# A branch moved from behind the last expert group to behind the sixth, its loads on another queue, and a shorter lead of split weights

## The chip, the core and the metric

The kernel is written in Bass with Tile for one core of a Trainium2 chip. The metric is device time in microseconds (us) of one execution; the time shown is the median of three runs. TensorE (PE) multiplies, VectorE (DVE) and ScalarE (ACT) do elementwise work, GpSimd (POOL) a little of it, and SyncE (SP) issues the DMAs. [...]

## What is computed

Two transformer blocks run one after the other on 256 tokens of width 1024, all in 32-bit floats. The first block ends in a mixture of experts: each token goes to two of 32 experts.

```python
def hierarchical_moe(h, w_rg, b_rg, w_re, b_re, w_gate, w_up, w_down):
    ...
    for g in range(N_GROUPS):
        sl = slice(g * EXPERTS_PER_GROUP, (g + 1) * EXPERTS_PER_GROUP)
        act = jax.nn.silu(jnp.einsum('nd,edf->nef', h, w_gate[sl])) * jnp.einsum('nd,edf->nef', h, w_up[sl])
        act = act * combine[:, g, :, None]
        y = y + jnp.einsum('nef,efd->nd', act, w_down[sl])
    return y
```

The second block has projections, attention and a gated unit side by side, an output projection, a layer norm, a dense feed-forward net (`swiglu_ffn`) and a second layer norm.

```python
def hybrid_mixer(x, w_in, attn_out_g, gmlp_out_g, gmlp_ln_g, gmlp_ln_b, w_spatial, b_spatial, w_out):
    h = x @ w_in
    q, k, v, u, z = jnp.split(h, [A, 2 * A, 3 * A, 3 * A + G], axis=-1)
    ...
    merged = jnp.concatenate([rms_norm_2(attn, attn_out_g), rms_norm_2(sg, gmlp_out_g)], axis=-1)
    return merged @ w_out
```

## The kernel before, in words

**Weights.** All weights come from HBM in tiles of 1 MB (128 partitions x 2048 floats). `Feed` (lines 53 to 88) keeps one fixed order of tiles and a list of free slots; whenever a slot is given back with `done`, `pump` issues the next load on SP's queue (line 77). While the experts run there are 23 slots; behind them only the six of `ring1` stay, and only those may take tiles of block 2. SP has at most eight tiles on the way at once: a load waits for the landing of the load eight before it.

**Experts.** The 32 experts run in eight groups of four (`g` from 0 to 7, lines 810 to 868). Each expert has room for 32 tokens. A group takes eight "gu" tiles (gate and up, line 806), then gathers the tokens of the next group (`picks`, `gather`, `some` with line 755 on PE and line 756 on DVE; `scatter` with line 763 on DVE and line 768 on PE), then `h` (lines 836, 837), its transpose (line 841, 842), four "dn" tiles (line 806 again) and the way back to tokens (`to_tokens`, line 847), which adds into the PSUM banks `acc`. In the last group `warm` (line 231) puts 12 recorded small matmuls behind nearly every tile. PE works in program order here; on ACT and DVE the scheduler chooses the order.

**Branch.** More than 32 tokens for one expert are handled in a body behind a branch on a value that the router computed (lines 872 to 911). With these inputs the body is not entered. It stands behind the last group. Five engines load the value (line 873) and each takes its own branch (line 874). In the program's listing the body holds 1233 instructions of PE, 263 of ACT, 192 of SP, 75 of DVE and one of POOL. The way around it brings the semaphores to where the body would have left them: one such instruction on PE, ACT and DVE, each of which waits for that engine's own work, and eight on SP, one for each of the eight tiles on the way, since the body's loads go through SP; none on POOL. Then each engine jumps to the code behind.

**Block 2.** Weights are used as a high and a low part of 32 bits each: `hi_lo` (lines 258 and 259) makes `whi` on ACT and `wlo` on DVE, for a unit of half a tile. `Split` (lines 91 to 117) makes units ahead of their use: `get` asks that `n` units, `WBUF2` = 9, be made beyond those used, and there are buffers for nine. After the experts, `acc` is split into `xh`, `xl` (lines 1090 to 1095, in program order on PE, ACT, DVE and POOL), and five projections follow, `z2`, `q2`, `k2`, `u2`, `v2`, each with four units and two rows of tokens (`proj_tok`, matmuls on line 271: 12 for each unit), with steps of other work between the units. `z_scale` (984 on DVE; 985, 986 on POOL) and `z_mix` (line 992 on PE) stand in `k2`. Attention's `soft_a` to `soft_e` stand in `v2` and the output projection `wo2`. The feed-forward net has 22 hidden slices; `first_hidden` (lines 1218, 1221) makes the first two, line 1247 asks for nine units ahead, and `hidden` (lines 286, 287) and `gated` (lines 1255 to 1262) do the rest; a hidden slice needs the PSUM banks that an earlier `gated` reads.

Of the kernel before, what the change touches and what calls it, by code (L numbers as in the profile page):

```python
# [32 lines left out]
RINGX = 4  # L33
WBUF = 3
# [18 lines left out]
class Feed:  # L53


    def __init__(self, nc, order):
        self.nc = nc
        self.order = order
        self.free = []
        self.loaded = []  # L60
        self.n_loaded = 0
        self.slot = {}
# [5 lines left out]
    def pump(self):  # L68
        while self.n_loaded < len(self.order):
            name, src, stage = self.order[self.n_loaded]  # L70
            fit = [i for i, s in enumerate(self.free) if s[1] >= stage]
            if not fit:
                return
            s = self.free.pop(fit[0])
            t = s[0].tile([P, 2048], F32, tag="w", name="w")
            for c, part in src if isinstance(src, list) else [(slice(0, 2048), src)]:
                self.nc.sync.dma_start(out=t[:, c], in_=part)
            self.loaded.append((name, t, s))
            self.n_loaded += 1
# [11 lines left out]
class Split:  # L91


    def __init__(self, feed, pool, units, hi_lo, n):
        self.feed, self.pool, self.units, self.hi_lo, self.n = feed, pool, units, hi_lo, n
        self.held = {}
        self.ready = []
        self.n_got = 0
# [13 lines left out]
    def get(self, name, less=0):  # L112
        self.ahead(self.n_got + self.n - less)
        got, hi, lo = self.ready[self.n_got]
        assert got == name, (got, name)
        self.n_got += 1
        return hi, lo
# [3 lines left out]
def fused_blocks(ctx: ExitStack, tc: tile.TileContext, a, out):  # L121
# [47 lines left out]
    for g in range(NG):  # L169
        tiles(None, "gu", [a["w_gu"][g, k] for k in range(KD)], MOE)  # L170
        tiles(None, "dn", [a["w_dn"][g, j] for j in range(4)], MOE)
    for n, i in (("z2", 4), ("q2", 0), ("k2", 1), ("u2", 3), ("v2", 2)):
# [118 lines left out]

    def proj_tok(W, name, xh, xl, then={}, new=bank):
        accs = [[new()] for _ in range(NT)]
        for u in range(4):
            hi, lo = W.get(name)
            for t in range(NT):
                dense_tok(accs[t], [(2 * u, hi, lo, 0), (2 * u + 1, hi, lo, 512)], (0,), xh, xl, t, u == 0, u == 3)
            if u in then:
                W.ahead(W.n_got + W.n)
                then[u]()  # L300
        return [c[0] for c in accs]

    def rows_proj(W, name, acc, xh, xl, k0, first, last, then={}):

        if not last:
            for u in range(2):
# [3 lines left out]
                if u in then:  # L310
                    W.ahead(W.n_got + W.n)
# [498 lines left out]
    with tc.manual_schedule(engines={mybir.EngineType.PE}):  # L810
        for g in range(NG):
            end = g == NG - 1
            gu = bank_c()
            idle = bank_c() if end else None
            first = {0: ((0, 1), (1, 1)), 1: ((2, 2),), 2: ((4, 4),)} if g == 0 else {}
            for kc in range(KD):
                for k in first.get(kc, ()):
                    some(*k)
                by_expert([gu], xg[:, kc, :], feed.get("gu"), kc == 0, kc == KD - 1)
                if end:  # L820
                    warm(lambda: idle, WARM2, ident)
            if not end:
                if g == 0:
                    st = scatter(0, pg)
                pg = picks(g + 1)
                xg, some = gather(pg)
                some(0, 4)
                some(4, 4)
                st_next = scatter(g + 1, pg)
            if g == 0:  # L830
                for kc in range(KD):
                    for t in range(NT):
                        mm(acc[kc // 2][:, kc % 2, t * P:(t + 1) * P], xres[:, t, kc * P:(kc + 1) * P], ident,
                           start=kc % 2 == 0 and t == 0, stop=False, skip_group_check=True)
            h = dp.tile([P, 256], F32, tag="pr", name="h")
            act(h, gu[:, 0:256], AF.Silu)  # L836
            tt(out=h, in0=gu[:, 256:512], in1=h, op=ALU.mult)
            hT = dp.tile([P, 2, P], F32, tag="pg", name="hT")
            za = bank_c()[:, 0:256]
            for f in range(2):  # L840
                tr(za[:, f * P:(f + 1) * P], h[:, f * P:(f + 1) * P], ident)
            act(hT, za.rearrange("p (f s) -> p f s", f=2), AF.Copy)  # L842
            ys = []

            def to_tokens(c):
                for k in range(4):
                    mm(acc[2 * c + k // 2][:, k % 2, :], ys[c][:, k * P:(k + 1) * P], st, start=False, stop=False,  # L847
                       skip_group_check=True)

            for c in range(2):  # L850
                zy = [bank_c() for _ in range(1 + (end and c))]
                for f in range(2):
                    by_expert(zy, hT[:, f, :], feed.get("dn"), f == 0, f == 1)
                    if c and not f:
                        to_tokens(0)
                    elif end and not c:
                        warm(lambda: idle, WARM2, ident)
                y = dp.tile([P, 512], F32, tag="y", name="y")
                if c and end:
                    act(y[:, 0:256], zy[0][:, 0:256], AF.Copy)  # L860
                    nc.vector.tensor_copy(y[:, 256:512], zy[1][:, 0:256])
                elif c:
                    nc.vector.tensor_copy(y, zy[0])  # L863
                else:
                    act(y, zy[0], AF.Copy)
                ys.append(y)
            to_tokens(1)
            st = st_next
    r2es.close()


    oes, op_ = pool("over", side="right")
    n_over = nc.values_load(over[0:1, 0:1], min_val=0, max_val=S)
    with tc.If(n_over > 0):
        late = op_.tile([P, NT, NE], F32, name="late")
        stt(out=late, in0=pos, scalar=float(SLOT + 1), in1=comb, op0=ALU.is_ge, op1=ALU.mult)
        xT = [op_.tile([P, KD, P], F32, name=f"x1T{t}") for t in range(NT)]
        oT = op_.tile([P, 2, S], F32, name="oT")
        ow = [op_.tile([P, 4, 512], F32, name=f"ow{i}") for i in range(2)]
        for t in range(NT):  # L880
            for b in range(2):
                act(xT[t][:, 4 * b:4 * b + 4, :], x1_t(t, b), AF.Copy)
            ts(late[:, t, :], late[:, t, :], rs[t], None, op0=ALU.mult)
            tt(out=xT[t], in0=xT[t], in1=V("ffn_g").unsqueeze(2).to_broadcast([P, KD, P]), op=ALU.mult)
        for e in range(NE):
            g, i = divmod(e, GE)
            gps = [bank_c() for _ in range(NT)]
            for j in range(2):
                w = ow[(3 * e + j) % 2]
                src = a["w_gu"][g, 4 * j:4 * j + 4].rearrange("k p (e f) -> p e k f", e=GE)  # L890
                nc.sync.dma_start(out=w, in_=src[:, i])
                for k in range(4):
                    kc = 4 * j + k
                    for t in range(NT):
                        mm(gps[t], xT[t][:, kc, :], w[:, k, :], start=kc == 0, stop=kc == KD - 1)
            for t in range(NT):
                so = op_.tile([P, 256], F32, tag="so", name="so", bufs=2)
                act(so, gps[t][:, 0:256], AF.Silu, scale=rs[t])
                stt(out=so, in0=gps[t][:, 256:512], scalar=late[:, t, e:e + 1], in1=so,
                    op0=ALU.mult, op1=ALU.mult)  # L900
                za = bank_c()[:, 0:256]
                for f in range(2):
                    tr(za[:, f * P:(f + 1) * P], so[:, f * P:(f + 1) * P], ident)
                act(oT[:, :, t * P:(t + 1) * P], za.rearrange("p (f s) -> p f s", f=2), AF.Copy)
            w = ow[(3 * e + 2) % 2]
            nc.sync.dma_start(out=w, in_=a["w_dn"][g].rearrange("x p (e f) -> p e x f", e=GE)[:, i])
            for kc in range(KD):
                for f in range(2):
                    mm(acc[kc // 2][:, kc % 2, :], w[:, 2 * (kc // 4) + f, (kc % 4) * P:(kc % 4 + 1) * P],
                       oT[:, f, :], start=False, stop=False, skip_group_check=True)  # L910
    oes.close()
# [8 lines left out]
    W = Split(feed, wp, units_b, hi_lo, WBUF2)  # L920
# [191 lines left out]
    nc.scalar.preload_act_table_set("natural_log_exp_and_others")  # L1112
    b2["v2"] = proj_tok(W, "v2", xh, xl, then([(z_gate, 0), (soft_b, 0)], [(soft_a, 1), (z_gate, 1), (soft_c, 0)],
# [59 lines left out]
    with tc.manual_schedule(engines=in_order):  # L1173
# [73 lines left out]
        W.ahead(W.n_got + W.n)  # L1247
# [149 lines left out]
```

## Time and profile before

| | |
|---|---|
| median of 3 runs | 714.85 us (713.87 to 716.04) |
| the profiled execution's own time | 713.62 us |
| its span, first to last instruction | 711.9 us |
| mean granted PE clock in it | 0.978 |
| PE busy | 661.3 us, 93% |
| DVE busy | 368.2 us, 52% |
| ACT busy | 271.1 us, 38% |
| POOL busy | 43.9 us, 6% |
| DMA | 185.63 MB, mean 261 GB/s |

The profile is one execution of the program. All positions below are us from the start of its span. A windows row gives the stretch, its length, then for PE, PE's weight loads (PEld), DVE, ACT and POOL the busy us with the number of instructions, then the granted PE clock, the DMA engines' share and GB/s. A timeline row gives start, busy us (of all instructions merged into the row), engine, line, operation, output and inputs, count, and in brackets the idle time before it with what ended it. An engine's name with a q (PEldq, SPq) is its instruction queue: branches and semaphore instructions show there.

### The profile page before, as it was taken

Reading aid. Unit: us, or ns where it says so; the run is one execution under the profiler, and the core shown is the slowest. Engines: PE = TensorE matmul, PEld = TensorE weight load, DVE = VectorE, ACT = ScalarE, POOL = GpSimd, SP = SyncE. Lnnn points to the kernel's source line nnn. Section 1 sums busy time; section 2 is a strip of 40 time slices with the busy share of each in tenths; the row PEclk is TensorE's granted clock in tenths of the full one; section 3 lists DMA queues with packets and bytes.
Section 4 is the critical chain, followed back from the end, with each engine's and each line's share of the span. In section 5 each row is a group of like instructions: output and inputs, shape, how many; then the busy total and the mean of one; then the engine's idle time right before and its main releaser. Section 6 shows DMA issues by size and latency. Waiting matters only on the chain. (4 is left out here: it accounts for less than half of the span.)

```text
span 711.9 us, 10413 instructions
## 1 busy us (share of the span) xinstructions
PE 661.3 (93%) x4249; PEld 516.7 (73%) x4249; DVE 368.2 (52%) x578; ACT 271.1 (38%) x413; POOL 43.9 (6%) x60
## 2 busy tenths in 40 slices
PE   8999999999999888998799598999979999999995
PEld 6888999999964444434256386877778888888884
DVE  6657555555521211212000488577578767667646
ACT  6567554444310000000000583477364444444410
POOL 2321100000000000000000006001100000000001
PEclk9999999999999999999899799999999999999998
DMA  8983479738879999999999784542146655555001
GB/s 341 410 338 119 147 303 347 258 122 344 365 298 394 421 420 419 419 420 417 418 418 416 269 319 155 193 162 66 54 180 234 231 189 192 200 193 178 1 0 60
DMA packets 27558, 185.63 MB, mean 261 GB/s; under 512 B 3312, under 2 KB 3824, under 8 KB 5872
## 3 DMA queue, kind: packets, MB, share of 16 engines
q1 hardware_dynamic: 27504, 184.89, 67.2%
q8 instruction: 36, 0.59, 0.3%
q14 instruction: 18, 0.15, 0.1%
HBM read 183.83 MB, written 1.05 MB: 260 GB/s over the span
## 5 line engine op out<-in xcount | busy, mean ns | idle before, releaser
L259 DVE TENSOR_TENSOR wlo<-w,whi 128x1024 fp32r<-128x1024 f32 (+1 forms) x151 | 185.4, 1237 | 84.3 <-ACT whi L258 83.1
L258 ACT ACTIVATE whi<-w 128x1024 fp32r<-128x1024 f32 (+1 forms) x151 | 157.3, 1057 | 165.9 <-PE pa_t L271 67.9
L286 PE MATMUL pc_t<-x,whi 128*128 128x512 f32 x320 | 114.9, 402 | 3.8 <-DVE fs L1255 3.8
L287 PE MATMUL pc_t<-x,wlo 128*128 128x256 f32 x320 | 90.4, 282 | 0.0
L286 PEld LDWEIGHTS pc_t<-x,whi 128*128 128x128 f32 x320 | 60.8, 190 | 19.0 <-ACT fs L1256 4.1
L806 PE MATMUL pc_t<-w,xg 128*32 128x512 f32 x512 | 62.0, 617 | 4.0 <-DMA w<-in_w_gu_dram 4.0
L287 PEld LDWEIGHTS pc_t<-x,wlo 128*128 128x128 f32 x320 | 61.1, 191 | 0.4
L836 ACT ACTIVATE h<-pc_t 128x256 f32<-128x256 f32 x8 | 3.1, 384 | 135.2 <-PE pc_t L755 110.5
L756 DVE TENSOR_TENSOR xg<-pc_t,vec 128x512 f32<-128x512 f32 (+2 forms) x18 | 11.4, 633 | 80.2 <-PE pc_t L755 80.2
L806 PEld LDWEIGHTS pc_t<-w,xg 128*32 128x32 f32 x512 | 14.5, 111 | 39.6 <-issue 26.0
L271 PE MATMUL pa_t<-whi,x 128*128 128x512 f32 x128 | 42.8, 403 | 0.0
L847 PEld LDWEIGHTS pa_t<-st,y 128*128 128x128 f32 x128 | 23.0, 189 | 21.9 <-DVE y L863 12.5
L847 PE MATMUL pa_t<-st,y 128*128 128x256 f32 x128 | 31.9, 392 | 6.3 <-DVE y L863 6.2
L280 PE MATMUL pc_t<-xh,wlo 128*128 128x256 f32 x128 | 36.2, 283 | 0.0
L279 PE MATMUL pc_t<-xl,whi 128*128 128x256 f32 x128 | 36.2, 283 | 0.0
L278 PE MATMUL pc_t<-xh,whi 128*128 128x256 f32 x128 | 36.2, 283 | 0.0
L806 PE MATMUL pc_t<-w,hT 128*32 128x512 f32 (+1 forms) x272 | 31.2, 574 | 4.1 <-ACT hT L842 4.1
L755 PEld LDWEIGHTS pc_t<-pr,xres 128*128 128x128 f32 x256 | 29.3, 192 | 7.8 <-PE pc_t L806 4.2
L755 PE MATMUL pc_t<-pr,xres 128*128 128x128 f32 x256 | 31.1, 278 | 0.9 <-DVE pr L746 0.9
L863 DVE COPY y<-pc_t 128x512 f32<-128x512 f32 x7 | 4.8, 692 | 50.8 <-PE pc_t L806 50.8
L271 PE MATMUL pa_t<-whi,fh 128*128 128x512 f32 x88 | 28.7, 392 | 0.0
L271 PE MATMUL pa_t<-wlo,fh 128*128 128x512 f32 x88 | 28.6, 391 | 0.0
(313 smaller groups left out, 1225.6 us busy)
## 6 DMA issues: line engine op xcount, KB each, us to landing
w<-in_w_gu_dram SPq DMA_DIRECT2D x64, 1024.0 KB, 19.4
w<-in_w_dn_dram SPq DMA_DIRECT2D x32, 1024.0 KB, 19.6
w<-in_w_in_dram SPq DMA_DIRECT2D x28, 1024.0 KB, 12.6
w<-in_w_ffn_dram SPq DMA_DIRECT2D x22, 1024.0 KB, 4.9
w<-in_w_fdn_dram SPq DMA_DIRECT2D x11, 1024.0 KB, 4.8
w<-in_w_out_dram SPq DMA_DIRECT2D x8, 1024.0 KB, 5.0
w<-in_w_in_dram SPq DMA_DIRECT2D x4, 512.0 KB, 12.2
w<-in_w_cv_dram SPq DMA_DIRECT2D x2, 1024.0 KB, 9.4
```

The costliest lines, as they stand in the source:

```text
L258: act(hi, src, AF.Copy)
L259: tt(out=lo, in0=src, in1=hi.bitcast(F32), op=ALU.subtract)
L271: mm(acc[c], x_[:, kc, tok], w_[:, o + c * 512:o + (c + 1) * 512], start=first and i == 0 and n == 0, stop=last and i == len(ks) - 1 and n ...
L278: mm(acc, hi[:, f], xh[:, kc, :], start=kc == 0, stop=False)
L279: mm(acc, hi[:, f], xl[:, kc, :], start=False, stop=False)
L280: mm(acc, lo[:, f], xh[:, kc, :], start=False, stop=kc == nk - 1)
L286: mm(z, hi[:, f], x[:, :, kc, :], start=kc == 0, stop=False, skip_group_check=True)
L287: mm(z[:, 0, :], lo[:, f], x[:, 0, kc, :], start=False, stop=kc == nk - 1, skip_group_check=True)
L755: mm(zv[:, k, :], xres[:, t, kc * P:(kc + 1) * P], pr[:, t, :], start=t == 0, stop=t == 1)
L756: tt(out=xg[:, ks, :], in0=zv, in1=V("ffn_g")[:, ks].unsqueeze(2).to_broadcast([P, n, P]), op=ALU.mult)
L806: mm(out[sl, 0:n], x[:, sl], w[:, e * 512 + i * n:e * 512 + (i + 1) * n], start=start, stop=stop, skip_group_check=True)
L847: mm(acc[2 * c + k // 2][:, k % 2, :], ys[c][:, k * P:(k + 1) * P], st, start=False, stop=False, skip_group_check=True)
```

## The change

The loop over the groups becomes a function `group`, with the same steps. Groups 0 to 5 run as before; then comes the branch, now `overflow`; then groups 6 and 7 run in program order on PE, ACT, DVE and POOL (`in_order`). The body takes its memory from two slots of the weight rings ("room" entries in the order of tiles, which load nothing), handles one row of 128 tokens after the other (so it is longer on PE and loads the weights twice), and issues its loads on GpSimd's queue. It holds no instruction for SP. `Split` gets a lead that is apart from its nine buffers: five units in `z2` to `u2`; from `v2` on one more with every `get`, up to nine; behind `first_hidden` it is set to two and grows again, in place of the request for nine on line 1247.

```diff
@@ class Feed
-            for c, part in src if isinstance(src, list) else [(slice(0, 2048), src)]:
+            for c, part in src if isinstance(src, list) else [(slice(0, 2048), src)] if src is not None else []:
@@ class Split
-    def __init__(self, feed, pool, units, hi_lo, n):
+    def __init__(self, feed, pool, units, hi_lo, n, lead=None):
...
+        self.lead = lead or n
+        self.grow = 0
...
     def get(self, name, less=0):
-        self.ahead(self.n_got + self.n - less)
+        self.lead = min(self.n, self.lead + self.grow)
+        self.ahead(max(self.n_got + 1, self.n_got + self.lead - less))
@@ the order of tiles
         tiles(None, "dn", [a["w_dn"][g, j] for j in range(4)], MOE)
+        if g == G_OVER:
+            tiles(None, "room", [None, None], MOE)
@@ proj_tok, rows_proj
-                W.ahead(W.n_got + W.n)
+                W.ahead(W.n_got + W.lead)
@@ the experts
+    def overflow():
+        rooms = [feed.get("room") for _ in range(2)]
...
+        n_over = nc.values_load(over[0:1, 0:1], min_val=0, max_val=S)
+        with tc.If(n_over > 0):
...
+            for t in range(NT):
...
+                for e in range(NE):
...
+                        nc.gpsimd.dma_start(out=w, in_=src[:, i])
...
+        for r in rooms:
+            feed.done(r)
+
+    state = pg, xg, some, None
+    for gs in (range(G_OVER + 1), range(G_OVER + 1, NG)):
+        with tc.manual_schedule(engines={mybir.EngineType.PE} if gs[0] == 0 else in_order):
+            for g in gs:
+                state = group(g, *state)
+        if gs[0] == 0:
+            overflow()
     r2es.close()
...
-    n_over = nc.values_load(over[0:1, 0:1], min_val=0, max_val=S)
-    with tc.If(n_over > 0):
...
-                nc.sync.dma_start(out=w, in_=src[:, i])
...
@@ block 2
-    W = Split(feed, wp, units_b, hi_lo, WBUF2)
+    W = Split(feed, wp, units_b, hi_lo, WBUF2, WBUF + 2)
@@ behind u2
+    W.grow = 1
     b2["v2"] = proj_tok(W, "v2", xh, xl, then([(z_gate, 0), (soft_b, 0)], [(soft_a, 1), (z_gate, 1), (soft_c, 0)],
@@ behind first_hidden
-        W.ahead(W.n_got + W.n)
+        W.lead = 2
```

## Rows read from the trace of the kernel before

**Rows 1.** the page, 40 slices: busy share of PE and DMA in tenths.

```profile
PE   8999999999999888998799598999979999999995
...
DMA  8983479738879999999999784542146655555001
```

**Rows 2.** windows around three idle spells of PE (columns below).

```profile
395.00:403.50 8.50, 0.02 (x1) 0.00 (x0) 2.68 (x4) 2.60 (x6) 0.00 (x0) 0.66 0.66 267
...
403.50:408.30 4.80, 4.77 (x12) 3.81 (x13) 3.65 (x6) 4.80 (x9) 0.00 (x0) 0.54 0.67 220
...
437.60:440.84 3.24, 0.01 (x1) 0.00 (x0) 3.24 (x2) 1.06 (x1) 3.11 (x2) 1.00 0.66 278
...
440.84:445.90 5.06, 5.06 (x23) 4.57 (x24) 2.32 (x3) 0.00 (x0) 2.54 (x2) 0.66 0.00 0
...
530.80:534.56 3.76, 0.00 (x1) 0.03 (x1) 3.76 (x6) 2.95 (x5) 0.00 (x0) 0.95 0.99 377
...
534.56:537.60 3.04, 3.04 (x9) 2.64 (x10) 3.04 (x7) 1.06 (x3) 0.00 (x0) 0.50 0.68 278
```

**Rows 3.** line 874, the branch, per queue: ns min/median/max, first and last start.

```profile
L874 PEldq COMPARE_BRANCH  x1: 6152/6152/6152, 394.1 to 394.1; - x1
...
L874 POOLq COMPARE_BRANCH  x1: 45/45/45, 394.4 to 394.4; - x1
...
L874 SPq EVENT_SEMAPHORE  x8: 17/17/17, 394.8 to 402.6; - x8
...
L874 PEldq EVENT_SEMAPHORE  x1: 51/51/51, 400.3 to 400.3; - x1
```

**Rows 4.** line 271 from 400 us: PE's first instruction behind the branch.

```profile
L271 PEldq EVENT_SEMAPHORE  x1: 51/51/51, 403.4 to 403.4; - x1
```

**Rows 5.** the chain that ended last, in order of time, where block 2 begins.

```profile
400.41 0.39 ACT x L258
...
403.53 7.76 PE pc_t L271 x24
...
411.74 2.74 PE pc_t L271 x12
```

**Rows 6.** timeline of DVE ahead of the second spell and of the third.

```profile
433.31 2.35 DVE L259 TENSOR_TENSOR wlo<-w,whi 128x1024 fp32r<-128x1024 f32 x1 [0.23 <-ACT whi L258]
...
436.18 0.68 DVE L984 TENSOR_TENSOR z<-z,rs 128x512 f32<-128x512 f32 x1
...
523.44 9.18 DVE L259 TENSOR_TENSOR wlo<-w,whi 128x1024 fp32r<-128x1024 f32 x8 [0.52 <-ACT whi L258]
```

**Rows 7.** timeline (start us, us) of PE, groups 5 to 7.

```profile
333.70 2.78 PE L806 MATMUL pc_t<-w,xg 128*32 128x512 f32 x24
...
337.33 1.07 PE L806 MATMUL pc_t<-w,xg 128*32 128x512 f32 x8 [0.84 <-DMA w<-in_w_gu_dram]
...
342.31 1.93 PE L806 MATMUL pc_t<-w,xg 128*32 128x512 f32 x8 [0.56 <-DMA w<-in_w_gu_dram]
...
348.29 3.84 PE L755 MATMUL pc_t<-pr,xres 128*128 128x128 f32 x32
...
362.77 1.06 PE L806 MATMUL pc_t<-w,xg 128*32 128x512 f32 x8
...
363.77 1.60 PE L231 MATMUL pc_t<-ident 128*128 128x128 f32 x12
```

**Rows 8.** timeline of group 5: steps that group 6 repeats.

```profile
323.09 0.69 DVE L756 TENSOR_TENSOR xg<-pc_t,vec 128x512 f32<-128x512 f32 x1 [1.10 <-PE pc_t L755]
...
324.26 0.41 PE L841 MATMUL pc_t<-ident,h 128*128 128x128 f32 x2 [0.99 <-DVE h L837]
...
332.60 0.43 DVE L763 TENSOR_TENSOR pg<-pg,wr 128x256 f32<-128x256 f32 x1
```

**Rows 9.** the page's DMA issues: KB each, median us from issue to landing.

```profile
w<-in_w_gu_dram SPq DMA_DIRECT2D x64, 1024.0 KB, 19.4
```

**Rows 10.** windows again: the attention stage of block 2.

```profile
471.00:485.00 14.00, 14.00 (x75) 10.84 (x73) 10.83 (x29) 10.86 (x31) 0.69 (x1) 1.00 0.38 123
```

More of the change, by code (lines that the diff above doesn't have):

```diff
@@ L33 @@
 RINGX = 4
+G_OVER = 5
 WBUF = 3
@@ L310, in rows_proj @@
                 if u in then:
-                    W.ahead(W.n_got + W.n)
+                    W.ahead(W.n_got + W.lead)
                     then[u]()
@@ L808, in by_expert @@
         feed.done(w)
[L810 to L815, printed above, removed]
-            for kc in range(KD):
[L817 to L820, printed above, removed]
-                    warm(lambda: idle, WARM2, ident)
[L822 to L868, printed above, removed]
@@ L869, in fused_blocks @@
-    r2es.close()
-    oes, op_ = pool("over", side="right")
-    n_over = nc.values_load(over[0:1, 0:1], min_val=0, max_val=S)
-    with tc.If(n_over > 0):
[L875 to L890, printed above, removed]
-                nc.sync.dma_start(out=w, in_=src[:, i])
[L892 to L910, printed above, removed]
@@ L911, in fused_blocks, with group, to_tokens @@
-    oes.close()
+    def group(g, pg, xg, some, st):
+        end = g == NG - 1
+        gu = bank_c()
+        idle = bank_c() if end else None
+        first = {0: ((0, 1), (1, 1)), 1: ((2, 2),), 2: ((4, 4),)} if g == 0 else {}
+        for kc in range(KD):
+            for k in first.get(kc, ()):
+                some(*k)
+            by_expert([gu], xg[:, kc, :], feed.get("gu"), kc == 0, kc == KD - 1)
+            if end:
+                warm(lambda: idle, WARM2, ident)
+        if not end:
+            if g == 0:
+                st = scatter(0, pg)
+            pg = picks(g + 1)
+            xg, some = gather(pg)
+            some(0, 4)
+            some(4, 4)
+            st_next = scatter(g + 1, pg)
+        if g == 0:
+            for kc in range(KD):
+                for t in range(NT):
+                    mm(acc[kc // 2][:, kc % 2, t * P:(t + 1) * P], xres[:, t, kc * P:(kc + 1) * P], ident,
+                       start=kc % 2 == 0 and t == 0, stop=False, skip_group_check=True)
+        h = dp.tile([P, 256], F32, tag="pr", name="h")
+        act(h, gu[:, 0:256], AF.Silu)
+        tt(out=h, in0=gu[:, 256:512], in1=h, op=ALU.mult)
+        hT = dp.tile([P, 2, P], F32, tag="pg", name="hT")
+        za = bank_c()[:, 0:256]
+        for f in range(2):
+            tr(za[:, f * P:(f + 1) * P], h[:, f * P:(f + 1) * P], ident)
+        act(hT, za.rearrange("p (f s) -> p f s", f=2), AF.Copy)
+        ys = []
+        def to_tokens(c):
+            for k in range(4):
+                mm(acc[2 * c + k // 2][:, k % 2, :], ys[c][:, k * P:(k + 1) * P], st, start=False, stop=False,
+                   skip_group_check=True)
+        for c in range(2):
+            zy = [bank_c() for _ in range(1 + (end and c))]
+            for f in range(2):
+                by_expert(zy, hT[:, f, :], feed.get("dn"), f == 0, f == 1)
+                if c and not f:
+                    to_tokens(0)
+                elif end and not c:
+                    warm(lambda: idle, WARM2, ident)
+            y = dp.tile([P, 512], F32, tag="y", name="y")
+            if c and end:
+                act(y[:, 0:256], zy[0][:, 0:256], AF.Copy)
+                nc.vector.tensor_copy(y[:, 256:512], zy[1][:, 0:256])
+            elif c:
+                nc.vector.tensor_copy(y, zy[0])
+            else:
+                act(y, zy[0], AF.Copy)
+            ys.append(y)
+        to_tokens(1)
+        return None if end else (pg, xg, some, st_next)
@@ L1246, in fused_blocks @@
             first_hidden(1, j)
-        W.ahead(W.n_got + W.n)
+        W.lead = 2
     acc = None
```

35 lines of the change are left out of this document (added).

## The prediction, made before the changed kernel ran

> **What bounds the kernel now.** First the page's 40 slices [rows 1]: PE is at eight or nine tenths nearly everywhere, and where the experts run (slices 12 to 22) DMA is at nine. So time can only be won where PE stands idle or runs at the lower clock, and in the experts' stage only as far as the loads allow. Then windows around PE's idle spells [rows 2]; the reader is to see three in which PE is busy for 0.02 us or less: 395.0 to 403.5 (8.5 us) where the branch stands, 437.6 to 440.84 (3.24 us) ahead of `z_mix`, and 530.8 to 534.56 (3.76 us) at the start of the feed-forward net. [...] The change touches all three.
>
> The first spell is PE's own. Its compare-and-branch takes 6152 ns [rows 3] and its semaphore instruction comes at 400.3; the first instruction behind the second jump comes at 403.4 [rows 4], 3.1 us later. ACT's split of `acc` began at 400.41 [rows 5], and the first matmul started at 403.53, as soon as PE was there. POOL, whose body is one instruction, took 45 ns. SP's eight semaphore instructions run from 394.8 to 402.6, spread over the landings of the eight tiles on the way, and until the last one SP issues nothing.
>
> In the second spell DVE is busy for all of 3.24 us [rows 2]: `z_scale` came at 436.18 behind a `wlo` of 2.35 us [rows 6], and POOL and PE follow from it. In the third DVE is busy for all of 3.76 us: eight `wlo` in a row from 523.44, 9.18 us [rows 6], stand ahead of the reductions in `gated` that give back the PSUM banks.
>
> **The branch behind the sixth group.** I take the same 8.5 us for PE's two jumps. The body grows, from the listing's 1233 PE instructions to 2 x (8 + 32 x 26) = 1680, but it is skipped, and was too long to be near before. [...] Its place is now the end of group 5, 333.7, so group 6's first gu tile starts at 342.2 and not at 333.70 [rows 7]. Before, PE took three tiles there in 2.78 us and then waited for the loads (0.84 at 337.33, 0.56 at 342.31), and reached the gather at 348.29. Now four or five tiles lie ready. At the lower clock one takes about 1.9 us (the row at 342.31), at the higher 0.93 (2.78 / 3). The lower clock lasted 4.8 us behind the branch [rows 2]; with 4.4 us of it, 2.4 tiles pass until 346.6, and 5.6 x 0.93 = 5.2 us bring PE to 351.8. So 8.5 us become **3.5 us** at the gather; the loads' slack pays for the rest. Ends: 0.5 and 8.5.
>
> The loads don't stop: eight tiles are on the way, and one takes 19.4 us from issue to landing [rows 9], over twice the hole. The two room slots are given back at the branch; in the order of tiles all but the last three loads of the experts stand ahead of it, so 21 slots in place of 23 cost nothing while eight limit SP. SP has no instruction in the body and nothing to make up for, so it should pass like POOL did; the eight waits go to POOL's own lanes, empty ones, and POOL has no work until block 2. If SP did wait, 8 us or more (394.8 to 402.6) would fall on the last three loads and the first of block 2.
>
> **Program order in groups 6 and 7.** DVE's `pg` step for the next scatter ran early before (332.60 [rows 8], ahead of the group's gu tiles). Now it stands behind the second `xg` (323.09 and 0.69 in group 5), and behind it on DVE wait `h` and through it PE's transpose (324.26 in group 5). The new chain from 323.8: `pg` 0.43, PE's transposes 0.41, then `st` and `h` on ACT and `h` on DVE at an estimated 0.4 each: 325.9 in place of 324.26, **1.7 us**. Low end 0 if that order is no worse. It occurs once: group 7 gathers nothing. Nor does group 7 make up for it: behind each tile stands 1.60 us of `warm` [rows 7], about 2.6 us a tile with the tile itself, and the loads come no faster (337.33 to 342.31 for two). So the last matmul moves from 395.0 to 395.0 + 3.5 + 1.7 = 400.2.
>
> **Into block 2.** Without a branch the first `z2` matmul needs one step on ACT (0.39 us [rows 5]) and some latency: 400.2 + 0.6 = 400.8 in place of 403.53, **-2.7 us**. The clock has no long gap to fall in. The first 24 matmuls took 7.76 us; at the later rate of 2.74 for 12 they take 5.48, -2.3; but the chain `x` on ACT and DVE, which ran beside slow matmuls, may now show: +0.8. **-1.5 us**, ends 0 and -2.3.
>
> **A lead of five.** By the time of `z_scale`, four units fewer have been split: at 9.18 / 8 = 1.15 us each [rows 6], 4.6 us of DVE. A split also no longer waits for PE to give back one of nine buffers, so it can fill DVE's idle time before. That is more than the 3.24 us of the spell, and the clock behind it, 5.06 us at 0.66, takes 1.7 us that the full clock would not. In full -4.9; but `rope` and `z_scale` still share one DVE queue whose order the scheduler draws up anew. I take **-3.5**; ends 0 and -4.9.
>
> From `v2` on the lead grows, four more splits (4.6 us of DVE) within attention, where DVE is busy 10.83 of 14 us and ACT 10.86 [rows 10]: the slack, 3.2 us in that stretch, nearly covers it, and units may be made in `u2`. **+0.5**; ends 0 and +4. If that cover is gone, the cost is PE's waits on softmax steps, and the clock with them.
>
> **A lead of two in the net.** The eight `wlo` of 9.18 us go from ahead of `gated` to behind it. PE wants the banks at 530.8 and had them at 534.56; with at most one `wlo` ahead of the reductions, 7 x 1.15 = 8 us go, so they are free in time. What is late next: the units. `hidden` asks for two with each `get` while the lead grows, so 4.6 us of DVE for each slice beside `gated`, and DVE was already full before and behind the spell (3.76 of 3.76 and 3.04 of 3.04 us [rows 2]). But a unit is used in the order in which it is made, and those asked for last are wanted last. Spell and lower clock behind it (3.04 us at 0.50, half of it lost) are 5.3 us; I take **-4.5**, ends -2 and -5.3.
>
> **Sum.** -2.7 - 1.5 - 3.5 + 0.5 - 4.5 = **-11.7 us** against the profiled execution's own 713.62 (span 711.9, so 1.7 us lie around it): 701.9. That execution is 1.2 us below the median of 714.85; I carry the difference over: **703.1**.
>
> [...]
>
> **Rivals.**
> *The hole is not absorbed.* Group 6's tiles come late or the lower clock lasts through it, so all 8.5 us reach the end: 5 us more, 708.1. For it: group 7 can't catch up. Against: the waits for loads in group 6 [rows 7].
> *The branch costs nothing there.* PE's jump goes as POOL's did, in 45 ns; the 3.5 us at the gather fall away: 699.6. Against: the 6152 ns of the same engine's jump, over a shorter body.
> *The leads do nothing.* Other splits take the places of those that go, and both later spells stay: -2.7 - 1.5 + 0.5 = -3.7, 711.1. For it: DVE is full in both spells, and its work in all stays the same. Against: what stands ahead of the late steps is splits for later.
> *The jumps wait behind the weights.* This one ends slower. PE's jump takes 5.4 us in which it does nothing, so it waits for something from outside; at 333.7 the DMA engines are fully taken, with eight tiles queued. If a jump waits as long as a tile, 19.4 us [rows 9] in place of 5.4, the end moves by 14 us: 717.1; if both do, 16.3 more, 733. It decides from a hole of about 20 us (8.5 + 11.7). For it: DMA's 9 in slice 19 [rows 1]. Against: at 394 tiles were landing at full pace too (SP's eight up to 402.6 [rows 3]), and the jump took 6.2 us.
>
> **Chances.** Forecast 0.63; not absorbed 0.13; branch free 0.05; leads do nothing 0.12; jumps behind the weights 0.06; 0.01 for others. The forecast's own ends, a few of them together, reach from 697.5 to 709. With the first rival and the third taken in, the range is **697.5 to 711**; the slower rival and a part of the third lie outside. A measurement of this kernel tells about 0.3% from no change, 2.1 us: faster (below 712.7) is the forecast and the first two rivals with most of the third, 0.91; no change 0.04; slower 0.05.
>
> **What would show each step.** PE's compare-and-branch near 334 with 5 to 6 us and group 6's first gu tile near 342; the gather near 352, not 348; group 7's first tile near 368, not 362.77; DMA at nine tenths throughout; SP's branch without landings to wait for. The last matmul of the experts near 400 and `z2` within 1 us of it at the full clock. No idle PE, or less than 1.5 us, ahead of `z_mix`; none at the second hidden slice; no new PE wait on attention's steps. The prediction is wrong if PE's hole is far from 8.5 us, if loads pause at the branch, if `z_mix` still waits for POOL, or if PE waits for `whi` or `wlo` in the net.

## The result, and the profile after

| | before | after |
|---|---|---|
| median, measured on one chip (5 runs each) | 713.97 us (713.73 to 716.04) | **708.9 us** (707.57 to 710.0) |
| the profiled execution's own time | 713.62 us | 707.57 us |
| its span | 711.9 us | 705.8 us |
| mean granted PE clock in it | 0.978 | 0.985 |

The ratio is 0.992, with a 95% interval of 0.9901 to 0.9939: faster by 4.4 to 7.1 us. The forecast was 703.1. The sign is right and the time lies in the range, but the forecast gain of 11.7 us has shrunk by half. Two of the three idle spells are gone as forecast; two new ones, which the prediction doesn't have, took the rest.

One remark for all positions below: the moment at which group 5 ends differs between profiled executions of different kernels by up to 3 us (332.1 to 334.9), with the same work ahead of it. Distances within one execution are therefore compared, and whole times by the timed runs. A granted clock is a share of PE's full speed: in the kernel before it is 1.00 over the tile that takes 1.07 us at 337.33 and 0.50 over the one that takes 1.93 at 342.31 [rows 7]; the second is what the text calls the lower clock.

**The branch.** The line of the branch in the kernel after, with the columns of [rows 3]:

```profile
L886 PEldq COMPARE_BRANCH  x1: 6052/6052/6052, 331.6 to 331.6; - x1
...
L886 PEldq EVENT_SEMAPHORE  x1: 51/51/51, 337.7 to 337.7; - x1
L886 SPq COMPARE_BRANCH  x1: 50/50/50, 359.6 to 359.6; - x1
```

PE's jump costs what it did (6152 ns before). SP has no semaphore instructions left there. What is new: 0.3 us behind PE's semaphore instruction PE works. The second pause, 3.1 us before [rows 3, 4], isn't there. In leads_alone below, with the branch at its old place, PE stands for 8.03 us, 3.05 more than the 4.98 here, so the pause seems to belong to that place; what it was there stays open.

**PE around it**, the timeline of PE in the kernel after:

```profile
331.01 1.99 PE L854 MATMUL pa_t<-st,y 128*128 128x256 f32 x8 [0.88 <-DVE y L870]
337.99 9.41 PE L814 MATMUL pc_t<-w,xg 128*32 128x512 f32 x64 [4.98 <-PEq L886]
347.32 3.84 PE L763 MATMUL pc_t<-pr,xres 128*128 128x128 f32 x32
352.28 0.44 PE L776 MATMUL pc_t<-ident,pg 128*128 128x128 f32 x2 [1.11 <-DVE pg L771]
354.01 0.41 PE L848 MATMUL pc_t<-ident,h 128*128 128x128 f32 x2 [1.30 <-DVE h L844]
...
363.46 1.07 PE L814 MATMUL pc_t<-w,xg 128*32 128x512 f32 x8
...
390.51 0.69 PE L848 MATMUL pc_t<-ident,h 128*128 128x128 f32 x2 [6.74 <-DVE h L844]
...
403.53 1.99 PE L854 MATMUL pa_t<-st,y 128*128 128x256 f32 x8
405.18 0.58 PE L279 MATMUL pc_t<-whi,x 128*128 128x512 f32 x1
```

The hole is 4.98 us. Behind it stand eight gate-and-up tiles in one row of 64 matmuls without a wait for a load, where before there were waits of 0.84 and 0.56 [rows 7]. The gather begins at 347.32, 14.3 us behind the end of group 5; before it was 348.29 behind 333.77 (331.78 and 1.99), 14.5. So the hole is paid for in full. Then come the two waits of program order (1.11 and 1.30). In group 7 the reader is to see the bracket of 6.74 us ahead of `h`'s transposes. What lies behind it shows in the timeline of ACT, kernel after:

```profile
357.00 0.60 ACT L872 ACTIVATE y<-pc_t 128x512 f32<-128x512 f32 x1 [2.10 <-PE pc_t L814]
387.81 1.06 ACT L266 ACTIVATE whi<-w 128x1024 fp32r<-128x1024 f32 x1 [30.21 <-DMA w<-in_w_in_dram]
388.77 0.37 ACT L843 ACTIVATE h<-pc_t 128x256 f32<-128x256 f32 x1
```

The first split of block 2, `whi` from `w_in`, stands **ahead of** group 7's `h` in ACT's queue. It waits 30.21 us for its tile to land, and `h`, DVE and PE wait with it. Before, the same instruction came behind the last copy of group 7; this is the timeline of ACT of the kernel before:

```profile
392.59 0.38 ACT L860 ACTIVATE y<-pc_t 128x256 f32<-128x256 f32 x1 [4.49 <-PE pc_t L806]
392.87 1.05 ACT L258 ACTIVATE whi<-w 128x1024 fp32r<-128x1024 f32 x1
```

**Windows** of the kernel after, columns as in [rows 2]:

```profile
383.77:390.51 6.74, 0.01 (x1) 0.00 (x1) 1.56 (x2) 1.33 (x2) 0.00 (x0) 0.75 1.03 417
390.51:397.35 6.84, 6.31 (x30) 3.33 (x30) 0.00 (x0) 0.38 (x1) 1.10 (x1) 0.50 1.02 414
...
405.18:410.80 5.62, 5.62 (x26) 4.62 (x25) 4.16 (x5) 5.62 (x10) 0.00 (x0) 1.00 0.50 172
437.00:446.00 9.00, 9.00 (x53) 7.77 (x52) 9.00 (x9) 3.44 (x5) 4.28 (x2) 1.00 0.56 189
502.09:504.60 2.51, 0.01 (x2) 0.01 (x1) 2.04 (x4) 0.87 (x2) 1.41 (x1) 1.00 0.73 225
...
524.00:538.00 14.00, 14.00 (x82) 12.21 (x81) 13.12 (x21) 11.45 (x17) 0.00 (x0) 1.00 0.43 150
```

The low clock behind the new spell falls on group 7's own tiles (0.50), and `z2` starts at the full clock (1.00, where it was 0.54 in [rows 2]). Ahead of `z_mix` and in the feed-forward net PE is busy for all of the window. But at 502.09, in layer norm 1, PE is idle for 2.5 us, and three more times up to 515.8. In the timeline of DVE there, kernel after:

```profile
500.50 1.23 DVE L267 TENSOR_TENSOR wlo<-w,whi 128x1024 fp32r<-128x1024 f32 x1
501.65 0.15 DVE L1176 TENSOR_SCALAR ve<-mv 128x1 f32<-128x1 f32 x1
501.87 1.23 DVE L267 TENSOR_TENSOR wlo<-w,whi 128x1024 fp32r<-128x1024 f32 x1
503.53 0.16 DVE L1197 SCALAR_TENSOR_TENSOR mr<-mv,rs 128x1 f32<-128x1 f32 x1 [0.44 <-POOL rs L257]
```

two `wlo`, for units that only `hidden` wants, stand between the steps of the layer norm that lead to PE's next transposes.

### The profile page after: what moved, and what is told of

The parts are those of the page before. It is cut to its first block, busy times and chain, and to the rows that moved or that the text cites. A ratio compares the mean times of both kernels' runs of the same rounds, so it can differ in the third digit from the quotient of the medians.

```text
span 705.8 us, 10415 instructions
## 1 busy us (share of the span) xinstructions
PE 656.4 (93%) x4249; PEld 513.5 (73%) x4249; DVE 367.4 (52%) x578; ACT 270.3 (38%) x413; POOL 46.0 (7%) x60
## 3 DMA queue, kind: packets, MB, share of 16 engines
HBM read 183.83 MB, written 1.05 MB: 262 GB/s over the span
```

## The experiments

The theory formed from this: the branch's own gain is eaten before `z2` by the queue of ACT (6.74 us and the clock behind it) and by program order; the leads win 10.2 us (4.9 and 5.3) and give 4.8 back in layer norm 1. Its rival is the prediction's sum. The table gives, for each kernel, the ratio to the kernel before, timed beside it on the same chip in five rounds. Three chips were used: one for branch_alone, leads_alone, one_section and ln_two, one for both, best, short_body and over6, one for order_pe_only, over6_fill3, best_fill3 and loads_sp; the kernel before took 715.69, 714.7 and 714.64 us there. So kernels of one chip are compared by their medians, and for kernels of different chips the difference of the ratios is given too.

| kernel | median us | ratio | 95% interval |
|---|---|---|---|
| after | 708.9 | 0.992 | 0.9901 to 0.9939 |
| branch_alone | 715.14 | 1.0001 | 0.9984 to 1.0019 |
| leads_alone | 709.33 | 0.9912 | 0.9893 to 0.9932 |
| one_section | 701.92 | 0.9804 | 0.9781 to 0.9826 |
| ln_two | 704.08 | 0.9839 | 0.9817 to 0.986 |
| both | 697.04 | 0.975 | 0.9736 to 0.9764 |
| best | 693.8 | 0.9702 | 0.9688 to 0.9716 |
| order_pe_only | 709.29 | 0.9933 | 0.9917 to 0.995 |
| short_body | 693.14 | 0.9713 | 0.9694 to 0.9733 |
| over6 | 701.96 | 0.9812 | 0.9798 to 0.9825 |
| over6_fill3 | 696.48 | 0.9745 | 0.9732 to 0.9759 |
| best_fill3 | 690.8 | 0.9667 | 0.9645 to 0.9688 |
| loads_sp | 694.59 | 0.9723 | 0.9703 to 0.9742 |

### The two halves of the change

**branch_alone**: the kernel after with the leads of before.

```diff
-    W = Split(feed, wp, units_b, hi_lo, WBUF2, WBUF + 2)
+    W = Split(feed, wp, units_b, hi_lo, WBUF2)
...
-    W.grow = 1
...
-        W.lead = 2
+        W.ahead(W.n_got + W.n)
```

> Branch and program order as in the changed kernel, weight lead as before (nine units ahead everywhere). Theory: the branch's gain is eaten before the dense layer starts, by the 30 us wait of the first weight split that stands ahead of the last group's silu on ScalarE (6.7 us of idle TensorE) and by 1.65 us of program order in the seventh group; z2's first matmul at 405 +-1 (403.53 before), full clock there, the two spells at 437 to 446 and 530 to 537 as before: 712 to 714, no difference that can be measured. Rival, the prediction's own terms (start 2.7 us earlier, 1.5 us of clock): z2's first matmul at 401, 709.8.

Measured: 1.0001, no difference. The timeline of PE of branch_alone shows the new wait and the two old ones, with `z2` starting at 405.42:

```profile
390.62 0.69 PE L848 MATMUL pc_t<-ident,h 128*128 128x128 f32 x2 [6.72 <-DVE h L844]
...
405.42 0.58 PE L279 MATMUL pc_t<-whi,x 128*128 128x512 f32 x1
...
441.09 0.66 PE L1010 MATMUL pc_t<-z,w 128*128 128x64 f32 x4 [2.60 <-POOL z L1004]
...
535.50 0.77 PE L294 MATMUL pc_t<-x,whi 128*128 128x512 f32 x1 [3.77 <-DVE fs L1273]
```

As made, the move of the branch is worth nothing.

**leads_alone**: the kernel before with the other half.

```diff
-    W = Split(feed, wp, units_b, hi_lo, WBUF2)
+    W = Split(feed, wp, units_b, hi_lo, WBUF2, WBUF + 2)
...
+    W.grow = 1
...
-        W.ahead(W.n_got + W.n)
+        W.lead = 2
```

> Branch where it was before, the weight lead alone as in the changed kernel. Theory: the spell at z_mix goes (-4.9), the one in the FFN goes (-5.3), layer norm 1 loses 4.8 us to splits that come into it: 708.5 +-1, nearly the whole of the change's gain. Rival, the prediction's terms for the leads without a cost in layer norm: 703.8. Rival, the leads matter only together with the earlier start: 712 or more.

Measured: 0.9912, the whole of the change's gain. The hole behind the experts is still there, and the gap in layer norm 1 as well; PE of leads_alone:

```profile
405.73 0.76 PE L274 MATMUL pc_t<-whi,x 128*128 128x512 f32 x1 [8.03 <-ACT x L261]
...
507.60 1.36 PE L1192 MATMUL pc_t<-ident,xn 128*128 128x128 f32 x8 [2.50 <-ACT xn L1185]
```

### What stands in the way

**one_section**: groups 6 and 7 and the start of `z2` in one program-ordered section, where the change has two.

```diff
-        with tc.manual_schedule(engines={mybir.EngineType.PE} if gs[0] == 0 else in_order):
-            for g in gs:
-                state = group(g, *state)
+        ses = ExitStack()
+        ses.enter_context(tc.manual_schedule(engines={mybir.EngineType.PE} if gs[0] == 0 else in_order))
+        for g in gs:
+            state = group(g, *state)
         if gs[0] == 0:
+            ses.close()
             overflow()
...
-    with tc.manual_schedule(engines=in_order):
-        W.ahead(1)
+    W.ahead(1)
...
+    ses.close()
```

> The last two groups and the start of the second block's first projection in one program-ordered section instead of two, so that the first weight split stands behind the last group's silu, product and copies on ScalarE and VectorE. Theory: the 6.74 us of idle TensorE before the last group's transposes falls to about 1 us, z2's first matmul at 398.5 +-1.5 instead of 405.2, the low clock at 387 to 397 shrinks: 700.5 to 703. Rival: it was the weights' stream that ended last, and another wait for a transfer takes the place: first matmul at 403 or later, 706 to 709.

Measured: 701.92, 7 us under the kernel after (8.3 by the ratios). ACT has `h` at once and `whi` where it was before the change, behind the last copy; the first fence is the timeline of ACT of one_section, the second that of PE:

```profile
386.73 0.38 ACT L843 ACTIVATE h<-pc_t 128x256 f32<-128x256 f32 x1 [24.72 <-PE pc_t L814]
...
397.98 1.05 ACT L266 ACTIVATE whi<-w 128x1024 fp32r<-128x1024 f32 x1
```

```profile
388.03 0.38 PE L848 MATMUL pc_t<-ident,h 128*128 128x128 f32 x2
...
399.78 0.58 PE L279 MATMUL pc_t<-whi,x 128*128 128x512 f32 x1
```

`z2` starts at 399.78, 1.3 us later than the middle of what was expected, in an execution whose group 5 ended 1.9 us later than in the kernel after. The queue of ACT was the cause; no transfer took its place.

**ln_two**: one line more in the kernel after, inside layer norm 1's ordered section.

```diff
         W.lead = 2
+        W.ahead(W.n_got + 2)
```

> The changed kernel with one line more: the two weight splits of the next two units are requested as the last step of layer norm 1's program-ordered section, and so stand behind its steps on ScalarE and VectorE. Theory: layer norm's four gaps (6.1 us) fall to about 1.3 us as before: 704 to 705.5. Rival: the splits are then late for the first hidden unit behind layer norm, a gap of 3 to 5 us moves there: 708 to 710.

Measured: 704.08, 4.8 us under the kernel after (5.8 by the ratios). Of layer norm's four gaps (2.50, 1.53, 1.15 and 0.93 us, 6.1 in all; the kernel before had 1.3) two of any size are left. PE of ln_two:

```profile
504.00 1.36 PE L1207 MATMUL pc_t<-ident,xn 128*128 128x128 f32 x8 [0.37 <-ACT xn L1200]
...
512.90 0.39 PE L1237 MATMUL pa_t<-x,whi 128*128 128x256 f32 x1 [0.93 <-DVE x L267]
```

So a lead of two costs nothing in the net, and its cost in layer norm was the place of the next splits, not their number.

**both**: one_section with the line of ln_two.

```diff
         W.lead = 2
+        W.ahead(W.n_got + 2)
```

> The one section for the last two groups and z2's start, and the two splits at the end of layer norm's section, together. Theory: the two gains lie in different stages and add: 701.9 less 4.8 = 697.1 +-1. Rival: the weights' transfers are reached in the feed-forward part once everything ahead of it is earlier, 700 or more.

Measured: 697.04, and 708.9 - 7.0 - 4.8 = 697.1. By the ratios the gains are 8.3 and 5.8 us and 12.1 together. So the two add within some 2 us; that the medians agree to 0.1 is luck.

### Program order

**order_pe_only**: the kernel after, without order on ACT, DVE and POOL in groups 6 and 7.

```diff
-        with tc.manual_schedule(engines={mybir.EngineType.PE} if gs[0] == 0 else in_order):
+        with tc.manual_schedule(engines={mybir.EngineType.PE}):
```

> The changed kernel with its last two groups in program order on TensorE alone, as before the change; the first weight split still stands ahead of the last group's silu on ScalarE. Theory: the seventh group's transposes come 1.65 us earlier and the idle time ahead of the last group's transposes grows by as much, since it ends with the landing of the first dense weights: z2's start and the time within 0.7 us of the changed kernel's 708.9. Rival: program order is on the path in the changed kernel too, 1.5 to 3 us under it.

Measured: 709.29, no difference from 708.9. PE reaches the seventh group's transposes 19.2 us behind the end of group 5 (332.91), in place of 21.0 (333.00 to 354.01), and waits the longer later. PE of order_pe_only, then ACT:

```profile
352.11 0.41 PE L848 MATMUL pc_t<-ident,h 128*128 128x128 f32 x2 [0.99 <-DVE h L844]
...
390.89 0.69 PE L848 MATMUL pc_t<-ident,h 128*128 128x128 f32 x2 [9.03 <-DVE h L844]
```

```profile
388.19 1.06 ACT L266 ACTIVATE whi<-w 128x1024 fp32r<-128x1024 f32 x1 [32.50 <-DMA w<-in_w_in_dram]
```

This also says what put `whi` there. It stands ahead of `h` with and without the order of groups 6 and 7, and did not where the branch stands between the groups and block 2 (the kernel before). What changed is that the branch no longer lies between them, so that the scheduler may draw the split forward.

**best**: both, with group 6 in program order on PE alone and the common section from group 7 on.

```diff
-    for gs in (range(G_OVER + 1), range(G_OVER + 1, NG)):
+    for gs in (range(G_OVER + 1), range(G_OVER + 1, NG - 1), range(NG - 1, NG)):
...
-        ses.enter_context(tc.manual_schedule(engines={mybir.EngineType.PE} if gs[0] == 0 else in_order))
+        ses.enter_context(tc.manual_schedule(engines=in_order if gs[0] == NG - 1 else {mybir.EngineType.PE}))
```

> As both, with program order on TensorE alone for the seventh group, and the order on all engines from the last group on. Theory: the 1.65 us that program order costs in the seventh group (two waits of 1.1 and 1.3 us before its transposes) comes back and reaches z2's start, since nothing waits for a transfer behind it: 1.2 to 1.7 us under both, about 695.6. Rival: TensorE then waits for the last group's weights instead, the same time as both.

Measured: 693.8, 3.2 us under both, twice what was expected. The transposes wait 0.99 us in place of 1.11 and 1.30, as expected. More shows in the next matmuls. In both, the two waits are followed by the lower clock (granted 0.75 from 353.79 to 360.50) and 24 matmuls of the dn tiles take 4.48 us; in best, and in the kernel after, at full clock (1.00 from 354.90 to 358.00 in the latter), they take 2.78. PE of both, then of best:

```profile
355.09 0.41 PE L848 MATMUL pc_t<-ident,h 128*128 128x128 f32 x2 [1.30 <-DVE h L844]
356.02 4.48 PE L814 MATMUL pc_t<-w,hT 128*32 128x512 f32 x24 [0.52 <-ACT hT L849]
```

```profile
360.31 1.04 PE L814 MATMUL pc_t<-w,xg 128*32 128x512 f32 x2 [1.35 <-DMA w<-in_w_gu_dram]
```

These are 1.65 and 1.7 us, but they don't both reach `z2`, since the rival occurred in part: best waits 1.35 us for the first tile of group 7. From the end of group 5 to the start of `z2` it takes 62.22 us (332.88 to 395.10) and both 63.63 (334.50 to 398.13), 1.4 us more, which is what was expected. The other 1.6 us between the two executions lie ahead of the end of group 5, where the kernels do the same work. What makes up the rest of the 3.2 us stays open.

### The hole at the branch

**short_body**: best with a body for one expert; the handling of overflow for the other 31 is left out.

```diff
-                for e in range(NE):
+                for e in range(1):
                     g, i = divmod(e, GE)
```

> As best, with a body for one expert in place of 32 (the handling of overflow for the other 31 experts is left out; it isn't entered). Theory: TensorE's jump of 6.05 us is the price of a far target, and falls under 1 us when the body is short; the hole at group 5's end goes, and so does the low clock behind it, but not the time, since TensorE made the hole up while it waited for weights: within 0.7 us of best. Rival: any taken jump of TensorE costs 6 us here, the hole stays at 5. Rival: the hole did cost time, 3.5 to 5 us under best.

Measured: 693.14 (0.9713 against 0.9702 for best), no difference. PE's jump in short_body, and PE behind it:

```profile
L886 PEldq COMPARE_BRANCH  x1: 353/353/353, 330.7 to 330.7; - x1
```

```profile
332.39 3.64 PE L814 MATMUL pc_t<-w,xg 128*32 128x512 f32 x32 [0.30 <-PEq L886]
337.33 1.07 PE L814 MATMUL pc_t<-w,xg 128*32 128x512 f32 x8 [1.30 <-DMA w<-in_w_gu_dram]
...
346.68 4.80 PE L763 MATMUL pc_t<-pr,xres 128*128 128x128 f32 x32
```

Two things follow. The 6 us are the price of the long body: the same instruction takes 353 ns with a short one. Between the long bodies it doesn't grow (6152 ns over 1233 PE instructions, 6052 over 1680); at what length it begins no run here finds. And the hole costs no time where the change puts it: without it PE waits for loads instead, and the lower clock that follows those waits (granted 0.66 from 340 to 350) falls on the gather (4.80 us in place of 3.84).

**over6**: best with the branch one group later.

```diff
-G_OVER = 5
+G_OVER = 6
```

> As best, with the branch behind the seventh group instead of the sixth. Theory: TensorE makes up a hole of 5 us in any group with eight gate and up tiles behind it, since it takes a tile in 1.2 us that arrives every 2.45 us: z2's start and the time within 0.7 us of best. Rival: only with two groups behind it is there time to make it up, 3 to 5 us over best.

Measured: 701.96, **8.2 us over best**; the theory put it within 0.7. The hole is the same, but group 7 isn't like group 6: fillers stand behind its tiles. PE of over6:

```profile
349.31 5.78 PE L763 MATMUL pc_t<-pr,xres 128*128 128x128 f32 x32
...
370.73 1.93 PE L814 MATMUL pc_t<-w,xg 128*32 128x512 f32 x8 [4.93 <-PEq L886]
...
374.74 1.06 PE L814 MATMUL pc_t<-w,xg 128*32 128x512 f32 x8
...
377.27 1.06 PE L814 MATMUL pc_t<-w,xg 128*32 128x512 f32 x8
```

From tile to tile PE takes 2.53 us (374.74 to 377.27); a tile of 1.05 MB at 419 GB/s arrives every 2.50 us. There is nothing to make the hole up with. From the end of group 5 to the eighth tile of group 7 over6 takes 55.25 us (334.67 to 389.92) and best 48.03 (332.88 to 380.91), 7.2 us less. Of these, 4.9 are the hole, and 1.5 the lower clock behind it: the first tile with its fillers takes 4.01 us (370.73 to 374.74; granted 0.83 from 370 to 380). Some 0.8 lie ahead of the hole. There the gather comes behind waits for loads and takes 5.78 us, 1.94 more than in best, but best then waits 1.35 us for group 7's first tile. The last 1 us of the 8.2 isn't accounted for.

**over6_fill3** and **best_fill3**: the same test from the other side.

```diff
-WARM2 = 6
+WARM2 = 3
```

> As over6 (701.96), with three filler matmuls behind each gate and up tile of the last group in place of six. Theory: over6 lost the 5 us of its hole because a tile of the last group with its fillers takes TensorE 2.53 us while one arrives every 2.50 us, so that nothing can be made up; with three fillers a tile takes 1.86 us, and eight tiles make up some 5 us less what was no lag: 696.5 to 698.5. Rival: the hole's cost lies elsewhere (the low clock behind it, the stream), 700.5 or more.

Measured: 696.48, within what was expected, and 5.5 us under over6 (4.8 by the ratios). But this isn't the hole made up, since best gains by the same edit: over6_fill3 lies 5.7 us over best_fill3 (below), where over6 lay 8.2 over best. So three fillers fewer take 2.5 us off the price of the hole, and the greater part of it stays. PE of over6_fill3, then of best_fill3:

```profile
367.71 1.93 PE L814 MATMUL pc_t<-w,xg 128*32 128x512 f32 x8 [5.08 <-PEq L886]
...
382.56 1.06 PE L814 MATMUL pc_t<-w,xg 128*32 128x512 f32 x8
```

```profile
378.13 1.06 PE L814 MATMUL pc_t<-w,xg 128*32 128x512 f32 x8 [0.56 <-DMA w<-in_w_gu_dram]
```

In best_fill3 the eighth tile of group 7 starts as its load lands, 43.9 us behind the end of group 5 (334.28); in over6_fill3 it is 49.4 (333.16). A tile with three fillers takes 1.86 us there, 0.64 under the arrivals, but the first, at the lower clock, takes 3.44 (367.71 to 371.15). From the first tile to the eighth PE takes 14.85 us, where seven arrivals take 17.5: 2.65 us are made up, of a hole of 5.08 and the lower clock behind it.

> As best (693.8), with three fillers in place of six behind each tile of the last group. Theory: in best the last group's eighth tile starts some 3 us behind its arrival (first matmul at 380.9, first tile's wait ended at 360.3 and seven tiles of 2.50 us behind it come at 377.8); fewer fillers take most of that off: 690.5 to 692. Rival: TensorE then idles between tiles and z2 begins at the lower clock, 694 to 698.

Measured: **690.8**, the fastest of all, 3.3% under the kernel before and 3.0 us under best (2.5 by the ratios, whose intervals touch). `z2` starts at the full clock in it (its first matmul takes 0.58 us at 391.55, as in the kernel after at 1.00, where the kernel before takes 0.77 at 0.50), and PE waits for loads again in group 7 (0.57 and 0.56 us at 375.64 and 378.13). So half of the fillers stood on the path once everything ahead of them was mended.

**loads_sp**: best with the body's loads on SP's queue, as before the change.

```diff
-                        nc.gpsimd.dma_start(out=w, in_=src[:, i])
+                        nc.sync.dma_start(out=w, in_=src[:, i])
```

> As best (693.8), with the body's loads on SyncE's queue as before the change, the branch where the change puts it. Theory: SyncE then waits at its branch until the weight tiles that it has issued have landed (7.8 us of waits before the change), the weights' stream stops there, and TensorE waits for tiles behind it: 2 to 6 us over best, and a slice of the DMA row under 400 GB/s between 330 and 380. Rival: the ring holds enough, the time within 0.7 us of best.

Measured: 694.59, 0.9723 against 0.9702 for best: the intervals overlap, and the rival holds within what can be told. The mechanism did occur. The line of the branch on SP in loads_sp, and windows of loads_sp and of best:

```profile
L886 SPq EVENT_SEMAPHORE  x8: 17/17/17, 365.7 to 379.9; - x8
```

```profile
360.60:379.90 19.30, 19.30 (x145) 12.18 (x145) 0.00 (x0) 0.00 (x0) 0.00 (x0) 1.00 0.85 349
```

```profile
360.60:379.90 19.30, 19.30 (x140) 11.54 (x139) 0.00 (x0) 0.00 (x0) 0.00 (x0) 1.00 1.01 419
```

SP stands for 19.3 us until its eight tiles have landed, and the stream falls from 419 to 349 GB/s, 1.4 MB less. PE is busy for all of it: SP reaches its branch only when it has issued all but the last tiles of the experts, and what comes late are the last dn tiles, for which PE doesn't wait, and tiles of block 2. Of waits of PE that best doesn't have, only one of 1.11 us ahead of `z_mix` shows. What the change's other queue is worth here can't be told from nothing: 1.5 us by the ratios.

## Why the prediction was right or wrong

The terms beside what the two profiled executions show:

| step | forecast | measured |
|---|---|---|
| hole, at the gather of group 6 | +3.5 | -0.2 |
| program order in group 6 | +1.7 | +1.65 |
| group 7 | 0 | +6.7, and some 3 of low clock |
| start of `z2` | -2.7 | +1.65 |
| clock behind it | -1.5 | -2.0 |
| spell ahead of `z_mix` | -3.5 | -4.9 |
| growth of the lead in attention | +0.5 | not seen |
| spell in the net | -4.5 | -5.3 |
| layer norm 1 | 0 | +4.8 |
| sum (from the start of `z2` on) | -11.7 | -5.75, of 6.05 |

The start of `z2` is taken from the start of the span (405.18 and 403.53). From the end of group 5 it is +2.4 us, 72.18 against 69.76.

That the time lies in the range owes something to luck: terms that came out better than forecast (the hole, both spells) stand against two that the prediction doesn't have, group 7 and layer norm 1. The forecast number nearest to 708.9 is the 708.1 of the rival "the hole is not absorbed", and the hole was absorbed.

**The hole.** The mechanism was right, the size off. "I take the same 8.5 us for PE's two jumps": there was one pause of 4.98 us. The prediction names a hole far from 8.5 us as a sign of being wrong; of its ends at the gather, 0.5 and 8.5, the low one lay near what came, but why there is no second pause no run shows. With the hole over at 337.99 in place of 342.2, eight tiles brought PE to the gather 4.5 us sooner than worked out, and nothing was left of the 3.5. short_body shows that the end, too, doesn't feel it. The rival "the branch costs nothing there" thus has the right size at the gather for a wrong reason: the jump did take 6 us.

**Program order.** +1.65 for +1.7. But in the kernel after it is off the path, since the landing of `w_in` sets the end of group 7 (order_pe_only). Where nothing covers it, it costs 1.4 us at the start of `z2` (both and best).

**Group 7: the step that failed.** "So the last matmul moves from 395.0 to 395.0 + 3.5 + 1.7 = 400.2" took group 7 as it was. The prediction walked through what the change adds and moves within groups 5 to 7, but not through what the branch, when it left, set free to move: the first split of block 2, from another ordered section, stepped ahead of `h` on ACT and `wlo` ahead of `h`'s product on DVE (388.89 and 390.04). The wait for a landing at the head of a queue cost 6.74 us and, by the clock, some 3 us more (group 7's 0.50): from `h`'s transposes to the end of the last `to_tokens` it takes 15.0 us here (390.51 to 403.53 + 1.99) and 12.1 in one_section, which takes the split back. Of these 9.6 us one_section keeps 7.3 at the start of `z2` (64.85 us behind the end of group 5, in place of 72.18), since its group 7 comes 2.5 us later: the eighth tile at 50.66 us, in place of 48.17.

**Into block 2.** The latency forecast, 0.6 us behind the last matmul, was more than enough: `z2` began at 405.18 while the last `to_tokens` still ran (403.53 and 1.99). The clock came out near the full end of the term (24 matmuls in 5.80 us, 405.18 to 410.98, for what took 7.76; -2.0 of at most -2.3).

**The leads.** Both spells went in full, -10.2 for -8.0. The warning "z_mix still waits for POOL" did not come true. "What is late next" was asked in the net and answered there; it was the layer norm ahead of it that paid. The line that went, a request for nine units as the last step of an ordered section, had a second role: it kept those splits behind the layer norm. ln_two puts two of them back and gets the 4.8 us.

**The slower rival.** "The jumps wait behind the weights" didn't occur: with the stream at 408 GB/s from 331.6 to 337.7 the jump took 6.05 us. The growth of the lead (+0.5) wasn't separated by a run.

**The price of the jump.** PE's took 6052 ns over the long body (the kernel after) and 353 ns over the short one (short_body); those of POOL, SP, ACT and DVE took 45 to 72 ns in both. What PE waits for in it no run shows.

## What to carry to other kernels

When a branch, or a request at the end of an ordered section, is moved, ask for each engine what it held back: in the kernel after, a split of the second ordered section came ahead of `h` of the first in ACT's queue, and `h` stood behind it until its tile landed (30.21 us). PE's hole was free in group 6 (4.98 us in the kernel after), where a tile arrived every 2.50 us and PE took eight in 9.41 us, the lower clock included: the surplus per tile times the tiles behind it covered the hole. Fillers use that surplus up: in group 7 a tile took 2.53 us with six fillers and 1.86 with three, and the hole was not covered with either. A gain of 8 or 10 us at one place is only had after the next stage has been walked through as well.

## What was not expected of the hardware

A compare-and-branch of PE took between 5.99 and 6.15 us over the long body in before, after, one_section, both, best, over6 and loads_sp, whether group 5, 6 or 7 stood ahead of it, and 0.353 us over the short one. The hole moved the lower clock to a better place: with it, the clock granted in best is 0.80 over the first seven tiles of group 6 (337.85 to 346.28) and 1.00 from there into the gather (346.28 to 350.50); without it, in over6, it is 0.55 from 348.50 to 354.00, where the gather runs from 349.31 on and takes 5.78 us against 3.84. It needn't be so: in the kernel before, without the hole, the gather takes 3.84 us as well, and in short_body 4.80. A tiny `rs` on POOL took 1.57 us in the kernel after, with a `wlo` of DVE beside it, and 0.55 us in ln_two without one; that one is the cause was not tried.
